# A streaming kernel whose engine programs are shortened: waits and counts folded into arithmetic instructions, PE's groups in a loop, masks moved to Pool

## The chip, the cores and the metric

The kernel runs on one core of a Trainium2 chip. The metric is the device time of one execution in microseconds (us). Every run quoted here is fast: it lies within 1.5% of the fastest run of the same kernel. The engines are called VectorE (DVE in the profiles), ScalarE (ACT), Pool, PE (the matrix engine) and SyncE (SP); they wait for each other by semaphores, which are counters. Data is moved by 16 DMA engines. Comparisons are between kernels run on the same chip, except where the text says so.

## The reference

```python
def reference(x, w):                                # x: 8 x 2048 x 4096, w: 4096 x 1, float32
    proj = (x @ w).squeeze(-1)                      # 8 x 2048
    cm = np.maximum.accumulate(proj, axis=1)
    is_record = (proj >= cm).astype(np.float32)
    return np.cumsum(is_record, axis=1).astype(np.float32)
```

x holds 268 MB and is read once. Everything else is small.

## The kernel before

The rows of x are worked on in four groups, of 4, 4, 4 and 3 rows per partition, and a tail of 128 rows per batch. A group has eight tiles, one per batch. A tile is 128 partitions by `r` rows of 4096 numbers: 8.4 MB for a group of four rows, 6.3 MB for three. SyncE issues all loads of x, in order. Of each row VectorE multiplies and sums 2816 columns (one "dot"), Pool multiplies the other 1280 in place, and ScalarE sums what Pool wrote. When a tile is done, both VectorE and ScalarE have incremented its semaphore `fr[t]`, and the buffer may be loaded again. At the end of a group PE transposes the sums into PSUM, and VectorE runs the scans (maximum, comparison, count).

`at` picks the buffer by the tile's number within its group, since the engines run the groups as a loop and the same instruction must address the same buffer each time:

```python
NS = 3                                   # buffers; B = 8 tiles in a group, NL = 3 groups of four rows
def at(g, t):
    return xbuf[(t if g < NL else t + NS - 1) % NS]

def user_before(g, t):                   # whose release the load of tile t of group g waits for
    if t >= NS:
        return t - NS, g + 1
    if g == NL:
        return B - NS + t, g
    return max(u for u in range(B) if u % NS == t), g
```

The VectorE side, where a tile's wait also tells Pool to go, and the Pool side:

```python
def group_dots(r, g=0):                                   # VectorE
    for t in range(B):
        b, xb = B - 1 - t, at(g, t)
        V.wait_ge(xs[t], 16).then_inc(go, 1)              # landed; Pool may go
        V.sem_inc(xs[t], -16)
        for j in range(r):
            i = dot(xb[:, j * D : j * D + VC], w_v[:, :VC], sum_v[...])
        i.then_inc(fr[t], 1)
...
with V.Fori(0, NL - 1):                                   # two turns of a loop,
    next_group()
    group_dots(R)
next_group()                                              # a third copy written out
group_dots(R)
...
def group_products(r, g=0):                               # Pool
    for t in range(B):
        for j in range(r):
            xl = at(g, t)[:, j * D + VC : (j + 1) * D]
            i = G.tensor_mul(out=xl, in0=xl, in1=w_sb).then_inc(pl, 1)
            if j == 0:
                i._wait_ge(go, 1)
        G.sem_inc(go, -1)
```

In the tail the pieces of the last 128 rows run through the same three engines. Each sum is spread over batches by a small mask instruction (on ScalarE, the last one on VectorE) and added up on PE. Before the very last dot VectorE waits until ScalarE has done its last sum.

Of the kernel before, what the change touches and what calls it, by code (L numbers as in the profile page):

```python
# [13 lines left out]
ALU = mybir.AluOpType  # L14
ACTF = mybir.ActivationFunctionType
NEG = -3.0e38
LOW = -3.2e38
# [3 lines left out]
def kernel(  # L21
# [16 lines left out]
    P = 128  # L38
    B, S, D = x.shape
# [18 lines left out]
    LAST = [  # L58
        (B - 2, 1696, D, (1696, VC), (VC, D)),
        (B - 2, 0, 1696, (0, 1696), None),  # L60
        (B - 1, 2592, D, (2592, 3552), (3552, D)),
        (B - 1, 1440, 2592, (1792, 2592), (1440, 1792)),
        (B - 1, 736, 1440, (736, 1184), (1184, 1440)),
        (B - 1, 352, 736, (352, 736), None),
        (B - 1, 0, 352, (0, 352), None),
    ]
# [3 lines left out]
    TILES = [(m, 0, D, (0, VC), (VC, D)) for m in range(B - 2)] + LAST  # L70
    NP = sum(q[0] == B - 1 for q in LAST)
    EARLY = 4
    W2, W2C = 1184, 608

    pool = ctx.enter_context(tc.tile_pool(name="sb", bufs=1))
    wpool = ctx.enter_context(
# [37 lines left out]
    def sem(name):  # L114
        return tc.alloc_semaphore(f"{name}_{next(ns)}")
# [1 line left out]
    xs = [sem("xs") for _ in range(B)]  # L117
    fr = [sem("fr") for _ in range(B)]
    xq = [sem("xq") for _ in TILES]
    ws, idn, bw, wc, cs, od, oe, psr, pd, pl, go, sd, pa, con, fo, ms = (  # L120
        sem(n) for n in "ws idn bw wc cs od oe psr pd pl go sd pa con fo ms".split()
    )

    V, A, G, T, SY = nc.vector, nc.scalar, nc.gpsimd, nc.tensor, nc.sync
# [31 lines left out]
    def user_before(g, t):  # L156
# [3 lines left out]
            return B - NS + t, g  # L160
        return max(u for u in range(B) if u % NS == t), g

    with tc.tile_critical(no_gpsimd_drain=True):  # L163

        for g in range(NG):
            r = RS[g]
            for t in range(B):
                i = SY.dma_start(
                    out=at(g, t)[:, : r * D],
                    in_=x[B - 1 - t, STARTS[g] : STARTS[g] + r * P, :].rearrange(  # L170
                        "(p r) d -> p (r d)", r=r
                    ),
                ).then_inc(xs[t], 16)
                u, n = user_before(g, t)
                if n:
                    i._wait_ge(fr[u], 2 * n)
                if g == t == 0:
                    A.dma_start(
                        out=w_row, in_=w.rearrange("(k c) one -> k (c one)", k=NW)
                    ).then_inc(ws, 16)  # L180
                if t == 4 and g:
                    SY.dma_start(
                        out=out[:, STARTS[g - 1] : STARTS[g]], in_=cnt
                    )._wait_ge(cs, g + 1).then_inc(od, 16)
# [9 lines left out]
        for i, (m, c0, c1, _, _) in enumerate(TILES):  # L194
            u, xb = slot(m)
            d = SY.dma_start(  # L196
                out=xb[:, c0:c1],
                in_=x[
                    rows_of(m)[0] : rows_of(m)[0] + H,
                    S0 + rows_of(m)[1] : S0 + rows_of(m)[1] + Q, c0:c1,  # L200
                ].rearrange("b i d -> i b d"),
            ).then_inc(xq[i], 16)
            if u not in freed:
                freed.add(u)
                d._wait_ge(fr[u], 2 * NG)
            if i == len(TILES) - 4:
                SY.dma_start(
                    out=out[:, STARTS[-1] : S0], in_=cnt[:, : S0 - STARTS[-1]]
                )._wait_ge(cs, NG + 1).then_inc(oe, 16)
# [12 lines left out]
        for n, k in enumerate(order):  # L222
            c = k * WC
            dst = w_v[:, c : c + WC] if c < CV else ps
            i = T.matmul(  # L225
                out=dst, lhsT=identity[:NW, k : k + 1].to_broadcast([NW, P]),
                rhs=w_row, start=True, stop=True,
            ).then_inc(bw, 1)
            if n == 0:
                i._wait_ge(ws, 16)  # L230
        A.copy(out=w_sb[:, CV - VC :], in_=ps)._wait_ge(bw, 1).then_inc(wc, 1)  # L231
        A.copy(out=w_sb[:, : CV - VC], in_=w_v[:, VC:CV])._wait_ge(bw, NW).then_inc(  # L232
            wc, 1
        )
        A.copy(out=w2, in_=w_v[:, W2 : W2 + W2C]).then_inc(wc, 1)  # L235
        A.sem_inc(od, 32)


        V.wait_ge(idn, 1)
        V.memset(by_b, 0.0).then_inc(fo, 1)  # L240
        V.wait_ge(fo, 1)
        V.tensor_reduce(
            out=by_b[:, B - H : B], in_=identity.rearrange("p (i b) -> p b i", b=H),
            op=ALU.add,
            axis=mybir.AxisListType.X,
        )
        V.tensor_reduce(
            out=by_i, in_=identity.rearrange("p (i b) -> p i b", b=H), op=ALU.add,
            axis=mybir.AxisListType.X,
        ).then_inc(fo, 1)  # L250
        V.wait_ge(fo, 2)
        V.memset(cm[:, N - 1 :], NEG)
        V.memset(cnt[:, N - 1 :], 0.0)
        V.wait_ge(con, 3)
        V.wait_ge(wc, 3)
        V.memset(ps[:B, :N], LOW).then_inc(psr, 1)  # L256

        def group_scans(r=R):
            V.wait_ge(od, 16)
            n = r * P  # L260
            scans(cm[:, :n], cnt[:, :n], ps[:B, :n], cm[:, N - 1 :], cnt[:, N - 1 :])

        def group_dots(r, g=0):
            for t in range(B):
                b, xb = B - 1 - t, at(g, t)
                V.wait_ge(xs[t], 16).then_inc(go, 1)
                V.sem_inc(xs[t], -16)  # L267
                for j in range(r):
                    i = dot(
                        xb[:, j * D : j * D + VC], w_v[:, :VC],  # L270
                        sum_v[:, j * B + b : j * B + b + 1],
                    )
                i.then_inc(fr[t], 1)

        def next_group():
            group_scans()
            V.sem_inc(psr, -3)
            V.sem_inc(od, -16)

        with V.Fori(0, NL - 1):  # L280
            next_group()
            group_dots(R)
        next_group()
        group_dots(R)
        next_group()
        group_dots(RS[-1], NL)

        def group_products(r, g=0):
# [13 lines left out]
        def group_sums(r, g=0):  # L302
            for t in range(B):
                b = B - 1 - t
                for j in range(r):
                    i = add_up(
                        at(g, t)[:, j * D + VC : (j + 1) * D],
                        sum_p[:, j * B + b : j * B + b + 1],
                    )._wait_ge(pl, j + 1)
                i.then_inc(fr[t], 1)  # L310
                A.sem_inc(pl, -r)
            A.wait_ge(pd, 1)
            A.sem_inc(pd, -1)

        with A.Fori(0, NL):
            group_sums(R)
        group_sums(RS[-1], NL)

        for g, r in enumerate(RS):
            for j in range(r):  # L320
                for k, l in enumerate((sum_p, sum_v)):
                    i = T.matmul(  # L322
                        out=ps[:B, j : r * P : r], lhsT=l[:, j * B : (j + 1) * B],
                        rhs=identity, start=k == 0, stop=k == 1,
                    )
                    if j == k == 0:
                        i._wait_ge(fr[B - 1], 2 * (g + 1))
                    if j == r - 1:
                        i.then_inc((pd, psr)[k], 1)


        nv = npool = na = nm = 0

        def sums(i, dst_v, dst_p):
            nonlocal nv, npool, na
            m, _, _, v, p = TILES[i]
            xb = slot(m)[1]
            dot(xb[:, v[0] : v[1]], w_v[:, v[0] : v[1]], dst_v)._wait_ge(
                xq[i], 16
            ).then_inc(sd, 1)  # L340
            nv += 1
            if p:
                xl = xb[:, p[0] : p[1]]
                G.tensor_mul(out=xl, in0=xl, in1=w_pool(*p))._wait_ge(  # L344
                    xq[i], 16
                ).then_inc(pl, 1)
                npool += 1
                add_up(xl, dst_p)._wait_ge(pl, npool).then_inc(pa, 1)
                na += 1

        def by_batch(m, acc, start, stop, *wait):
            nonlocal nm
            e = masked[:, nm * B : (nm + 1) * B]
            b, q = rows_of(m)
            on = by_b[:, B - H - b : 2 * B - H - b]
            if m < B - 1:
                A.activation(out=e, in_=on, func=ACTF.Copy, scale=acc)._wait_ge(  # L357
                    *wait
                ).then_inc(ms, 1)
            else:  # L360
                V.tensor_tensor(
                    out=e, in0=on, in1=acc.to_broadcast([P, B]), op=ALU.mult
                )._wait_ge(*wait).then_inc(ms, 1)
            nm += 1
            return T.matmul(  # L365
                out=ps[:B, q : q + Q], lhsT=e, rhs=by_i, start=start, stop=bool(stop),
            )._wait_ge(ms, nm)

        def tail_scans(m0, m1, cm0, cnt0, base):
            a, b = (m * H * Q // B for m in (m0, m1))  # L370
            scans(cm_l[:, a:b], cnt_l[:, a:b], ps[:B, a:b], cm0, cnt0, base)

        A.wait_ge(fo, 2)
        n = RS[-1] * P
        for i, (m, c0, _, _, p) in enumerate(TILES[: -NP]):
            dv = acc_v[:, i : i + 1]
# [11 lines left out]
                tail_scans(0, EARLY, cm[:, n - 1 : n], cnt[:, n - 1 : n], 4)  # L388
        for j in range(NP):
            i = len(TILES) - NP + j  # L390
            if j == NP - 1:
                V.wait_ge(pa, na)
            sums(i, accs[:, j : j + 1], accs[:, NP + j : NP + j + 1])
        V.tensor_reduce(
            out=fin, in_=accs, op=ALU.add, axis=mybir.AxisListType.X
        )._wait_ge(sd, nv).then_inc(sd, 1)
# [36 lines left out]
```

## Time and profile before

The kernel before takes 633.26 us (median of 4 runs, 633.20 to 633.31).

The next lines are from the page of the kernel before. In the rows of digits each digit is the busy share of one fortieth of the span, in tenths; then come the DMA queues with packets, MB and their share of sixteen engines' time.

```profile
span 631.6 us, 1212 instructions
...
DVE  0755676456785557755579655577557866655797
...
POOL 0554676456765557755567655577555866555865
...
DMA  9999999999999999999999999999999999999995
...
q1 hardware_dynamic: 6560, 268.50, 98.6%
q14 instruction: 4, 0.03, 0.0%
q8 instruction: 1, 0.02, 0.0%
```

The DMA row is full from start to end: the kernel is bound by the load of x. VectorE (64%) and Pool (58%) have time to spare. The instruction queues carry almost nothing, five packets.

The timeline of the kernel before around the end of the first group, near 140 us: start, duration, engine, line, operation, and in brackets how long the engine had been idle. SPq is the issue of a load by SyncE.

```profile
140.19 11.50 POOL L292 TENSOR_TENSOR xall<-xall,w_sb 128x1280 f32<-128x1280 f32 x4 [7.86 <-POOLq L295]
140.33 3.09 DVE L127 CUSTOM_DVE_ANT_0 xall<-xall,w_v 128x2816 f32<-128x2816 f32 x1 [7.23 <-DVEq L267]
...
151.72 1.27 ACT L133 ACTIVATE xall<-xall 128x1280 f32<-128x1280 f32 x1 [1.50 <-POOL xall L292]
...
153.11 0.33 SPq L168 DMA_DIRECT2D xall<-in_x_dram  x1
```

A tile has landed at 140.06; Pool and VectorE start at once, ScalarE's last sum ends near 153.1, and in that moment SyncE issues the next load into the same buffer. So a buffer is free 13 us after landing. A tile takes 19.35 us to load.

The end of the kernel before, by the timeline: the scans of the last group, the last dot, and the reduction that starts the final chain.

```profile
599.52 1.00 DVE L143 TENSOR_TENSOR_SCAN cm<-ps,cm,small 8x384 f32<-8x384 f32 x1 [0.58 <-PE ps L322]
...
626.60 0.52 DVE L127 CUSTOM_DVE_ANT_0 xall<-xall,w_v 128x352 f32<-128x352 f32 x1 [0.35 <-ACT xall L133]
...
627.16 0.17 DVE L394 TENSOR_REDUCE small<-small 128x1 f32<-128x10 f32 x1
```

The last piece of x landed at 626.02 (the trace's landing records), and the reduction follows 1.14 us later.

### The profile page before, as it was taken

Reading aid. Unit: us, or ns where it says so; the run is one execution under the profiler, and the core shown is the slowest. Engines: PE = TensorE matmul, PEld = TensorE weight load, DVE = VectorE, ACT = ScalarE, POOL = GpSimd, SP = SyncE. Lnnn points to the kernel's source line nnn. Section 1 sums busy time; section 2 is a strip of 40 time slices with the busy share of each in tenths; the row PEclk is TensorE's granted clock in tenths of the full one; section 3 lists DMA queues with packets and bytes.
Section 4 is the critical chain, followed back from the end, with each engine's and each line's share of the span. In section 5 each row is a group of like instructions: output and inputs, shape, how many; then the busy total and the mean of one; then the engine's idle time right before and its main releaser. Section 6 shows DMA issues by size and latency. Waiting matters only on the chain.

```text
span 631.6 us, 1212 instructions
## 1 busy us (share of the span) xinstructions
PE 32.3 (5%) x108; PEld 14.4 (2%) x108; DVE 407.0 (64%) x295; ACT 182.0 (29%) x279; POOL 369.1 (58%) x138
## 2 busy tenths in 40 slices
PE   8000000000010000000020000000002000000111
PEld 3000000000000000000010000000001000000000
DVE  0755676456785557755579655577557866655797
ACT  1222332123322233222233222332222332322353
POOL 0554676456765557755567655577555866555865
PEclk9999999999999999999996555555556555555555
DMA  9999999999999999999999999999999999999995
GB/s 400 403 461 398 465 398 461 403 465 398 465 432 432 448 415 452 412 457 407 457 407 457 407 457 407 462 403 461 403 459 420 431 442 439 415 442 418 428 423 204
DMA packets 6581, 268.57 MB, mean 425 GB/s; under 512 B 768, under 2 KB 1040, under 8 KB 1584
## 3 DMA queue, kind: packets, MB, share of 16 engines
q1 hardware_dynamic: 6560, 268.50, 98.6%
q14 instruction: 4, 0.03, 0.0%
q8 instruction: 1, 0.02, 0.0%
q10 hardware_dynamic: 16, 0.02, 0.0%
HBM read 268.45 MB, written 0.07 MB: 425 GB/s over the span
## 4 chain that ended last, share of the span: by engine, by line
POOL 52%; issue 37%; DMA 7%; PE 2%; SPq 0%; DVE 0%; ACT 0%; POOLq 0%; ACTq 0%; DVEq 0%
POOL xall L292 52%; DMA xall<-in_x_dram 6%; PE w_v L225 2%; PE ps L225 0%; SPq L196 0%; DMA w<-in_w_dram 0%; POOL xall L344 0%; POOLq L295 0%; ACT xall L133 0%; ACT w L235 0%; DVE xall L127 0%; PE ps L365 0%; DVE cm_l L143 0%; DVE cnt_l L149 0%; DVE ps L146 0%
## 5 line engine op out<-in xcount | busy, mean ns | idle before, releaser
L127 DVE CUSTOM_DVE_ANT_0 xall<-xall,w_v 128x2816 f32<-128x2816 f32 (+3 forms) x133 | 388.4, 2973 | 190.1 <-DVEq L267 187.9
L292 POOL TENSOR_TENSOR xall<-xall,w_sb 128x1280 f32<-128x1280 f32 x120 | 344.8, 2903 | 248.5 <-POOLq L295 248.5
L133 ACT ACTIVATE xall<-xall 128x1280 f32<-128x1280 f32 (+1 forms) x130 | 162.9, 1253 | 425.5 <-POOL xall L292 415.1
L322 PE MATMUL ps<-identity,small 128*8 128x128 f32 x60 | 13.1, 409 | 569.7 <-ACT xall L133 569.7
L344 POOL TENSOR_TENSOR xall<-xall,w_sb 128x1280 f32<-128x1280 f32 (+1 forms) x8 | 21.6, 2709 | 7.3 <-DMA xall<-in_x_dram 7.3
L133 ACT ACTIVATION_READ_ACCUMULATOR xall<-xall 128x1 f32 x130 | 24.2, 186 | 0.0
L322 PEld LDWEIGHTS ps<-identity,small 128*8 128x8 f32 x60 | 7.4, 129 | 576.5 <-ACT xall L133 572.5
L143 DVE TENSOR_TENSOR_SCAN cm<-ps,cm,small 8x512 f32<-8x512 f32 (+1 forms) x5 | 6.1, 1218 | 13.2 <-PE ps L322 13.2
L225 PE MATMUL w_v<-w,identity 8*128 8x512 f32 x14 | 12.2, 1056 | 0.0
L256 DVE MEMSET ps<- 8x512 f32 x1 | 0.5, 485 | 16.0 <-ACT w L235 16.0
L127 DVE DVE_READ_ACCUMULATOR2_ANT small<- 128x1 f32 x133 | 10.8, 81 | 0.0
L365 PE MATMUL ps<-fold,masked 128*8 128x64 f32 x32 | 5.2, 299 | 23.3 <-ACT masked L357 17.3
L149 DVE TENSOR_TENSOR_SCAN cnt<-ps,cnt,small 8x512 f32<-8x512 f32 (+1 forms) x5 | 6.1, 1217 | 0.2
L357 ACT ACTIVATE masked<-fold,small 128x8 f32<-128x8 f32 x15 | 4.0, 296 | 4.1 <-DVE small L127 3.9
L225 PEld LDWEIGHTS w_v<-w,identity 8*128 8x128 f32 x14 | 4.6, 332 | 7.3 <-issue 7.3
L232 ACT COPY w_sb<-w_v 128x768 f32<-128x768 f32 x1 | 0.8, 798 | 11.4 <-PE w_v L225 11.4
L146 DVE TENSOR_TENSOR ps<-ps,cm 8x512 f32<-8x512 f32 (+1 forms) x5 | 3.3, 660 | 0.2
L365 PEld LDWEIGHTS ps<-fold,masked 128*8 128x8 f32 x32 | 1.9, 97 | 26.8 <-ACT masked L357 19.8
L225 PE MATMUL ps<-w,identity 8*128 8x512 f32 x2 | 2.1, 1136 | 2.6 <-DMA w<-in_w_dram 2.6
L231 ACT ACT_TABLE_LOAD x1 | 1.3, 1283 | 1.6 <-SPq L163 1.6
L344 POOL TENSOR_TENSOR xall<-xall,w 128x352 f32<-128x352 f32 (+1 forms) x2 | 1.6, 841 | 0.1
L231 ACT COPY w_sb<-ps 128x512 f32<-128x512 f32 x1 | 0.6, 585 | 1.9 <-PE ps L225 1.9
(22 smaller groups left out, 5.4 us busy)
## 6 DMA issues: line engine op xcount, KB each, us to landing
xall<-in_x_dram SPq DMA_DIRECT2D x8, 6144.0 KB, 33.5
xall<-in_x_dram SPq DMA_DIRECT2D x6, 2048.0 KB, 42.5
xall<-in_x_dram SPq DMA_DIRECT2D x1, 1200.0 KB, 36.7
xall<-in_x_dram SPq DMA_DIRECT2D x1, 848.0 KB, 38.1
xall<-in_x_dram SPq DMA_DIRECT2D x1, 752.0 KB, 39.3
xall<-in_x_dram SPq DMA_DIRECT2D x1, 576.0 KB, 40.1
xall<-in_x_dram SPq DMA_DIRECT2D x24, 45.1
xall<-in_x_dram SPq DMA_DIRECT2D x1, 352.0 KB, 22.5
```

The costliest lines, as they stand in the source:

```text
L127: return V.tensor_tensor_reduce(out=xsl, in0=xsl, in1=wsl, scale=1.0, scalar=0.0, op0=ALU.mult, op1=ALU.add, accum_out=dst,)
L133: return A.activation(out=xsl, in_=xsl, func=ACTF.Copy, accum_out=dst)
L143: V.tensor_tensor_scan(out=cm_, data0=src, data1=low, initial=cm0, op0=ALU.max, op1=ALU.max,)._wait_ge(psr, base).then_inc(psr, 1)
L146: V.tensor_tensor(out=src, in0=src, in1=cm_, op=ALU.is_ge)._wait_ge(psr, base + 1).then_inc(psr, 1)
L149: V.tensor_tensor_scan(out=cnt_, data0=src, data1=low, initial=cnt0, op0=ALU.add, op1=ALU.max,)._wait_ge(psr, base + 2).then_inc(cs, 1)
L225: i = T.matmul(out=dst, lhsT=identity[:NW, k : k + 1].to_broadcast([NW, P]), rhs=w_row, start=True, stop=True,).then_inc(bw, 1)
L231: A.copy(out=w_sb[:, CV - VC :], in_=ps)._wait_ge(bw, 1).then_inc(wc, 1)
L292: i = G.tensor_mul(out=xl, in0=xl, in1=w_sb).then_inc(pl, 1)
L322: i = T.matmul(out=ps[:B, j : r * P : r], lhsT=l[:, j * B : (j + 1) * B], rhs=identity, start=k == 0, stop=k == 1,)
L344: G.tensor_mul(out=xl, in0=xl, in1=w_pool(*p))._wait_ge(xq[i], 16).then_inc(pl, 1)
L357: A.activation(out=e, in_=on, func=ACTF.Copy, scale=acc)._wait_ge(*wait).then_inc(ms, 1)
L365: return T.matmul(out=ps[:B, q : q + Q], lhsT=e, rhs=by_i, start=start, stop=bool(stop),)._wait_ge(ms, nm)
```

## The change

Its intent is shorter engine programs. VectorE's separate wait and count instructions go into the arithmetic instructions beside them, and one such pair of ScalarE's becomes one instruction; VectorE runs the full groups as three turns of a loop instead of two and a copy; PE runs its groups in a loop, and the buffer of a group's last tile is given back through PE (semaphore `p7`), which also takes over VectorE's wait for the output of the counts (`od`); Pool makes six of the early masks of the tail; the wait for ScalarE moves from before the last dot to after it; and the split of two tail pieces shifts, by 32 and by 64 columns. The core of the diff:

```diff
-                V.wait_ge(xs[t], 16).then_inc(go, 1)
-                V.sem_inc(xs[t], -16)
                 for j in range(r):
                     i = dot(...)
+                    if j == 0:
+                        i._wait_ge(xs[t], 16).then_inc(go, 1)
+                    elif j == 1:
+                        i.then_inc(xs[t], -16)
                 i.then_inc(fr[t], 1)
...
-        with V.Fori(0, NL - 1):
-            next_group()
-            group_dots(R)
-        next_group()
-        group_dots(R)
-        next_group()
+        with V.Fori(0, NL):
+            group_scans()
+            V.sem_inc(psr, -3)
+            group_dots(R)
...
-        for g, r in enumerate(RS):
+        def group_rows(r):
+            T.wait_ge(fr[B - 1], 2).then_inc(p7, 1)
+            T.sem_inc(fr[B - 1], -2)
+            T.wait_ge(od, 16).then_inc(od, -16)
             ... (the matmuls of a group)
+        with T.Fori(0, NL):
+            group_rows(R)
+        group_rows(RS[-1])
...
+            pool = m < B - 2 and wait[0] is sd
+            if pool:
+                G.tensor_tensor(
+                    out=e, in0=on, in1=acc.to_broadcast([P, B]), op=ALU.mult
+                )._wait_ge(*wait).then_inc(mg, 1)
...
-            if j == NP - 1:
-                V.wait_ge(pa, na)
             sums(i, accs[:, j : j + 1], accs[:, NP + j : NP + j + 1])
+        V.wait_ge(pa, na)
```

More of the change, by code (lines that the diff above doesn't have):

```diff
@@ L60 @@
         (B - 2, 0, 1696, (0, 1696), None),
-        (B - 1, 2592, D, (2592, 3552), (3552, D)),
+        (B - 1, 2592, D, (2592, CV), (CV, D)),
         (B - 1, 1440, 2592, (1792, 2592), (1440, 1792)),
-        (B - 1, 736, 1440, (736, 1184), (1184, 1440)),
+        (B - 1, 736, 1440, (736, 1248), (1248, 1440)),
         (B - 1, 352, 736, (352, 736), None),
@@ L72 @@
     EARLY = 4
-    W2, W2C = 1184, 608
+    W2, W2C = 1248, 544
     pool = ctx.enter_context(tc.tile_pool(name="sb", bufs=1))
@@ L119 @@
     xq = [sem("xq") for _ in TILES]
-    ws, idn, bw, wc, cs, od, oe, psr, pd, pl, go, sd, pa, con, fo, ms = (
-        sem(n) for n in "ws idn bw wc cs od oe psr pd pl go sd pa con fo ms".split()
+    ws, idn, bw, wc, cs, od, oe, psr, pd, pl, go, sd, pa, con, fo, ms, p7, mg = (
+        sem(n) for n in "ws idn bw wc cs od oe psr pd pl go sd pa con fo ms p7 mg".split()
     )
@@ L161, in user_before, with free @@
         return max(u for u in range(B) if u % NS == t), g
+    def free(u, n):
+        return (p7, n) if u == B - 1 else (fr[u], 2 * n)
     with tc.tile_critical(no_gpsimd_drain=True):
@@ L175 @@
                 if n:
-                    i._wait_ge(fr[u], 2 * n)
+                    i._wait_ge(*(free(u, n)))
                 if g == t == 0:
@@ L204 @@
                 freed.add(u)
-                d._wait_ge(fr[u], 2 * NG)
+                d._wait_ge(*free(u, NG))
             if i == len(TILES) - 4:
@@ L230 @@
                 i._wait_ge(ws, 16)
+        A.wait_ge(fo, 2).then_inc(od, 16)
         A.copy(out=w_sb[:, CV - VC :], in_=ps)._wait_ge(bw, 1).then_inc(wc, 1)
@@ L235 @@
         A.copy(out=w2, in_=w_v[:, W2 : W2 + W2C]).then_inc(wc, 1)
-        A.sem_inc(od, 32)
-        V.wait_ge(idn, 1)
-        V.memset(by_b, 0.0).then_inc(fo, 1)
-        V.wait_ge(fo, 1)
+        V.memset(by_b, 0.0)._wait_ge(idn, 1).then_inc(fo, 1)
         V.tensor_reduce(
             out=by_b[:, B - H : B], in_=identity.rearrange("p (i b) -> p b i", b=H),
-            op=ALU.add,
-            axis=mybir.AxisListType.X,
-        )
+            op=ALU.add, axis=mybir.AxisListType.X,
+        )._wait_ge(fo, 1)
         V.tensor_reduce(
@@ L250 @@
         ).then_inc(fo, 1)
-        V.wait_ge(fo, 2)
-        V.memset(cm[:, N - 1 :], NEG)
-        V.memset(cnt[:, N - 1 :], 0.0)
-        V.wait_ge(con, 3)
-        V.wait_ge(wc, 3)
-        V.memset(ps[:B, :N], LOW).then_inc(psr, 1)
+        V.memset(cm[:, N - 1 :], NEG)._wait_ge(fo, 2)
+        V.memset(cnt[:, N - 1 :], 0.0)._wait_ge(con, 3)
+        V.memset(ps[:B, :N], LOW)._wait_ge(wc, 3).then_inc(psr, 1)
         def group_scans(r=R):
-            V.wait_ge(od, 16)
             n = r * P
@@ L272, in group_dots @@
                     )
+                    if j == 0:
+                        i._wait_ge(xs[t], 16).then_inc(go, 1)
+                    elif j == 1:
+                        i.then_inc(xs[t], -16)
                 i.then_inc(fr[t], 1)
-        def next_group():
+        with V.Fori(0, NL):
             group_scans()
             V.sem_inc(psr, -3)
-            V.sem_inc(od, -16)
-        with V.Fori(0, NL - 1):
-            next_group()
             group_dots(R)
-        next_group()
-        group_dots(R)
-        next_group()
+        group_scans()
+        V.sem_inc(psr, -3)
         group_dots(RS[-1], NL)
@@ L311, in group_sums @@
                 A.sem_inc(pl, -r)
-            A.wait_ge(pd, 1)
-            A.sem_inc(pd, -1)
+            A.wait_ge(pd, 1).then_inc(pd, -1)
         with A.Fori(0, NL):
@@ L325 @@
                     )
-                    if j == k == 0:
-                        i._wait_ge(fr[B - 1], 2 * (g + 1))
                     if j == r - 1:
                         i.then_inc((pd, psr)[k], 1)
-        nv = npool = na = nm = 0
+        with T.Fori(0, NL):
+            group_rows(R)
+        group_rows(RS[-1])
+        nv = npool = na = nm = on_a = on_g = 0
         def sums(i, dst_v, dst_p):
@@ L351, in by_batch @@
         def by_batch(m, acc, start, stop, *wait):
-            nonlocal nm
+            nonlocal nm, on_a, on_g
             e = masked[:, nm * B : (nm + 1) * B]
@@ L355, in by_batch @@
             on = by_b[:, B - H - b : 2 * B - H - b]
-            if m < B - 1:
+            pool = m < B - 2 and wait[0] is sd
[3 more added lines that the diff above has]
+                )._wait_ge(*wait).then_inc(mg, 1)
+            elif m < B - 1:
                 A.activation(out=e, in_=on, func=ACTF.Copy, scale=acc)._wait_ge(
@@ L364, in by_batch @@
             nm += 1
+            if pool:
+                on_g += 1
+            else:
+                on_a += 1
             return T.matmul(
                 out=ps[:B, q : q + Q], lhsT=e, rhs=by_i, start=start, stop=bool(stop),
-            )._wait_ge(ms, nm)
+            )._wait_ge(*((mg, on_g) if pool else (ms, on_a)))
         def tail_scans(m0, m1, cm0, cnt0, base):
@@ L371, in tail_scans @@
             scans(cm_l[:, a:b], cnt_l[:, a:b], ps[:B, a:b], cm0, cnt0, base)
-        A.wait_ge(fo, 2)
         n = RS[-1] * P
```

## The prediction

> **What bounds the kernel now.** The load of x. In the page's slices the DMA row reads 9 from first to last; q1 moves 268.5 MB at a mean of 425 GB/s, 98.6% of sixteen engines' span. The Trainium skill, "DMA: Bandwidth & Descriptors", section "Where 436 GB/s comes from", puts the port ceiling at 435 GB/s; the trace agrees (425). VectorE is busy 64%, Pool 58%, ScalarE 29%. By the timeline a steady tile of 4 rows lands every 19.4 us, and its buffer is free about 13 us after landing (four dots 12.1 us; four Pool products 11.5 us plus one ScalarE sum 1.5 us). Three buffers rotate, so a whole tile is always queued behind the one in flight. Only start and tail can therefore move the time: the last x lands near 626.0 us (estimate: 737 KB at 425 GB/s after 624.2), and the final chain follows.
>
> **What the change does.** Mid-stream it removes sequencer instructions, which sit in waits (VectorE sits idle 188 us before dots). It saves no stream time. The groups on PE as a loop move nothing. DVE's program shrinks from 235 to 168 rows in the instruction order.
>
> The important move is hidden: `go`, which releases Pool, was incremented by VectorE's wait as soon as the tile landed (Pool starts 0.14 us before the dot). Now it hangs on the first dot, and that inc sits on its accumulator read, 3.1 us later (dot 3.02 us start to start, read 0.08). Pool and ScalarE thus run 3.1 us later on every tile (more after a group's scans). Buffers come free about 16 us after landing instead of 13; within 19.4, and 13.2 within 14.5 for three-row tiles. The stream shouldn't notice.
>
> **The tail should.** Last group's last tile: the first dot starts at 586.8, so Pool starts at 589.95 instead of 586.67 and ends at 598.6; ScalarE ends at 599.8 (596.5 before); the twelve row matmuls take 2.75 us; the scans start at 602.95 instead of 599.52, with VectorE idle meanwhile. VectorE then has 22.7 us of back-to-back work; its old waits (0.9 + 0.63 + 0.31 us) absorb part, and taking the wait for ScalarE off the last dot gives back about 0.35. Last dot done at about 628.2 instead of 627.1.
>
> Pool's masks now wait for the dots: the mask of the sixth batch pair waits until about 621.6, so the next product runs 621.85 to 624.75 (before about 618.9 to 621.8). ScalarE's sum, three masks and three last sums follow in order: 626.15, 626.85, 627.6, 628.2, 628.65. VectorE's final wait clears at about 628.75; the final reduce, at 627.16 before, starts at about 628.8. Mask, matmul, scans and output are unchanged. Sum: +1.65 us, all on the final chain; the smaller last pieces (256 to 192 columns) are in that sum.
>
> **Prediction: 634.9 us, range 634.0 to 635.6.** Chance of faster by over 2%: 0.5%; within 2%: 99%; slower by over 2%: 0.5%.
>
> **What the profile would show.** DMA row unchanged, about 425 GB/s, last x piece landing at the same time. Pool's first product about 3.1 us after VectorE's first dot of each tile. VectorE idle some 4 us before the last group's scans, starting near 603. No DMA waits of VectorE from batch pair 5 on. The final reduce near 628.8, with ScalarE's last sum just ahead of it.
>
> **What would make it wrong.** If `go` rises at the first dot's start, the tail is about 0.3 us shorter than before: 633.0. If the later freeing of buffers makes a gap in the stream, it costs microseconds more. If Pool's small masks take over half a microsecond, or ScalarE's queue is slower than I added up, the tail grows further. Another chip's DMA rate could move both kernels.

## The result

The changed kernel takes 637.06 us (median of 4 runs, 636.89 to 637.42) against 633.26 of the kernel before: 3.8 us slower. The ratio is 1.0061, 95% interval 1.0043 to 1.0078. (A ratio here is the mean time of one kernel's fast runs over the mean of the other's in the same rounds, so not quite the ratio of the medians.) That is above the range of the prediction, 634.0 to 635.6, though well within 2%.

The page of the changed kernel, the same lines:

```profile
span 635.6 us, 1158 instructions
...
DVE  0855677455776557755568655676555986555787
...
POOL 0355775457736577555574655765457586665776
...
DMA  9999999999999999999999999999999999999994
...
q1 hardware_dynamic: 6560, 268.50, 98.2%
...
q14 instruction: 3, 0.02, 0.0%
```

The same bytes took a longer span, and two instruction packets are gone. The row of digits still looks full; a loss of 4 us in 635 can't be seen in it. The landing times of the tiles show it. This table is worked out from the trace's landing records; a tile has landed when its sixteenth increment is there.

```
                                         before     changed
last tile of group 1 landed at           159.42      158.90
first tile of group 2 after it           +19.34      +21.35
last tile of group 2 landed at           314.32      315.87
first tile of group 3 after it           +19.35      +21.54
last tile of group 3 landed at           469.22      473.16
first, second tile of group 4      +14.53, +15.50    +14.51, +14.54
last tile of group 4 landed at           586.54      589.43
last piece of x landed at                626.02      628.85
final reduction starts                   627.16      631.18
```

So the stream lost 2 us where group 2 begins and 2 us where group 3 begins, and won 1 us early in group 4; in group 1 the two traces differ by half a microsecond the other way. The tail after the last landing grew from 1.14 to 2.33 us. These sum up to 3.9 of the 4.0 us between the two spans.

The timeline of the changed kernel at the end of the first group:

```profile
139.58 3.09 DVE L127 CUSTOM_DVE_ANT_0 xall<-xall,w_v 128x2816 f32<-128x2816 f32 x1 [7.24 <-DMA xall<-in_x_dram]
142.75 11.48 POOL L285 TENSOR_TENSOR xall<-xall,w_sb 128x1280 f32<-128x1280 f32 x4 [7.88 <-POOLq L288]
...
154.26 1.27 ACT L133 ACTIVATE xall<-xall 128x1280 f32<-128x1280 f32 x1 [1.48 <-POOL xall L285]
...
155.65 0.33 SPq L171 DMA_DIRECT2D xall<-in_x_dram  x1
```

Pool starts 3.17 us after VectorE's first dot, where before it started 0.14 us ahead of it, and the next load is issued 16.1 us after the tile landed (139.56), not 13. The rate of the stream in the two stretches that hold the borders, first of the kernel before and then of the changed one: start and end, duration, busy us (and number of instructions) of PE, PE's weight loads, VectorE, ScalarE and Pool, and at the end the granted clock, the DMA share and GB/s. A packet's bytes count in the stretch in which it starts, so single stretches can exceed what the engines can move; the comparison is between the kernels.

```profile
155.00:185.00 30.00, 3.58 (x16) 1.97 (x16) 20.95 (x14) 7.14 (x11) 17.60 (x7) 1.00 1.04 450
...
305.00:345.00 40.00, 3.58 (x16) 2.04 (x16) 28.38 (x20) 11.00 (x18) 24.25 (x9) 0.87 1.02 442
```

```profile
155.00:185.00 30.00, 3.57 (x16) 1.98 (x16) 18.00 (x12) 6.08 (x10) 11.47 (x4) 1.00 1.00 419
...
305.00:345.00 40.00, 3.57 (x16) 2.05 (x16) 24.72 (x18) 9.54 (x14) 20.33 (x8) 1.00 1.00 419
```

At both borders between groups the rate falls. The packet records of the trace show why. How many of the 16 DMA engines had a packet in work, worked out from the starts and durations of the packets (mean of the quarter of a microsecond that begins there):

```
us               157.25  157.75  158.25  158.75  159.25
before             16.0    16.1    16.0    16.0    16.0
changed            16.0    12.0    11.0    14.6    16.0
```

In the changed kernel the first engines finish their part of the last tile of group 1 at 157.35. The next load was issued at 155.65, 1.7 us earlier, and its packets are not there for all of them: five engines stand still, the longest until 159.26. The first packets that they then move are slow: 2.5 to 3.6 us for 64 KB instead of 2.42. At the border to group 3 (312.9 to 314.0 us) it is worse, with as few as 6 of 16 at work.

The standing still is the smaller part of the loss. Near 160 us all 16 engines are at work again, and most packets still take 2.7 to 2.8 us. Added up over the engines (156 to 185 and 311 to 341 us), 17 us of engine time went in standing still and 33 us in packets that took longer than the usual 2.42 (64 KB) or 1.82 us (48 KB); in the kernel before both sums are nil, within 0.5 us. So here an issue that came too late cost more than the gap that it left.

The end of the changed kernel:

```profile
605.87 1.00 DVE L143 TENSOR_TENSOR_SCAN cm<-ps,cm,small 8x384 f32<-8x384 f32 x1 [4.30 <-PE ps L317]
...
630.50 0.50 DVE L127 CUSTOM_DVE_ANT_0 xall<-xall,w_v 128x352 f32<-128x352 f32 x1
...
630.63 0.35 ACT L133 ACTIVATE xall<-xall 128x192 f32<-128x192 f32 x1
...
631.18 0.16 DVE L398 TENSOR_REDUCE small<-small 128x1 f32<-128x10 f32 x1 [0.17 <-ACT xall L133]
```

VectorE waits 4.30 us for the last group's sums, which come late because Pool started late, and then works without a pause to the end of its last dot. ScalarE's last sum and VectorE's last dot end within 0.2 us of each other.

### The profile page after: what moved, and what is told of

Its sections match the earlier page's. It is cut to its first block, busy times and chain, and to the rows that moved or that the text cites. A ratio compares the mean times of both kernels' runs of the same rounds, so it can differ in the third digit from the quotient of the medians.

```text
span 635.6 us, 1158 instructions
## 1 busy us (share of the span) xinstructions
PE 32.2 (5%) x108; PEld 15.0 (2%) x108; DVE 406.6 (64%) x295; ACT 180.1 (28%) x273; POOL 369.2 (58%) x144
## 3 DMA queue, kind: packets, MB, share of 16 engines
HBM read 268.45 MB, written 0.07 MB: 422 GB/s over the span
## 5 line engine op out<-in xcount | busy, mean ns | idle before, releaser
L371 PEld LDWEIGHTS ps<-fold,masked 128*8 128x8 f32 x32 | 2.4, 110 | 24.0 <-ACT masked L359 16.1
L359 ACT ACTIVATE masked<-fold,small 128x8 f32<-128x8 f32 x9 | 2.5, 297 | 0.2
```

Source lines behind the costliest of these rows:

```text
L359: A.activation(out=e, in_=on, func=ACTF.Copy, scale=acc)._wait_ge(*wait).then_inc(ms, 1)
L371: return T.matmul(out=ps[:B, q : q + Q], lhsT=e, rhs=by_i, start=start, stop=bool(stop),)._wait_ge(*((mg, on_g) if pool else (ms, on_a)))
```

## The experiments

The theory: `go` now hangs on the completion of the first dot, so Pool, ScalarE and the release of every buffer are 3.1 us late. Within a group this costs nothing, since three tiles lie between two uses of a buffer and a whole tile is queued. But 8 is not a multiple of 3: tiles 7 and 8 of a group use the buffers that tiles 1 and 2 of the next group need, so at the border only two tiles lie between two uses, and there the release comes just before the DMA engines run out. The rivals: the hop of the last buffer's release over PE (`p7`), the loop on PE, and the masks on Pool. Names that begin with "a" are the changed kernel with an edit, those with "b" the kernel before with an edit. All results were correct.

### a1: go at the wait again

```diff
+                V.wait_ge(xs[t], 16).then_inc(go, 1)
                 for j in range(r):
                     i = dot(...)
-                    if j == 0:
-                        i._wait_ge(xs[t], 16).then_inc(go, 1)
-                    elif j == 1:
+                    if j == 1:
                         i.then_inc(xs[t], -16)
```

> The changed kernel with one thing undone: go is raised by VectorE's wait again, as soon as the tile landed; everything else of the change stays. Theory (buffers freed 3 us later starve the DMA queue where groups meet, about 2 us at each of the first two group borders, and the late Pool delays the tail): the border tiles land 19.4 us after the tile in front of them again, not 21.4 and 21.5, and the time falls from 637.1 to about 632.0 (631.4 to 632.6), below the kernel before, since one pair of instruction fetches less is in the stream. Rival (the extra hop over PE before the second buffer is given back, the PE loop, or Pool's masks): stays above 636.

Measured: 631.81 us (631.56 to 632.13), before 633.29, ratio 0.9975 (0.9959 to 0.9992). The first tiles of groups 2 and 3 land 19.34 and 19.35 us after the tile in front of them. One instruction per tile given back removes the whole loss, at the borders and in the tail, and the rest of the change is then worth 1.5 us in the other direction.

### b1: only the late go, in the kernel before

```diff
-                V.wait_ge(xs[t], 16).then_inc(go, 1)
-                V.sem_inc(xs[t], -16)
                 for j in range(r):
                     i = dot(...)
+                    if j == 0:
+                        i._wait_ge(xs[t], 16).then_inc(go, 1)
+                    elif j == 1:
+                        i.then_inc(xs[t], -16)
```

> The kernel before with only this part of the change: the wait moves into the first dot, go hangs on the first dot, the reset on the second. Theory (late go is the cause): both borders lose about 2 us of stream, the time is 637 to 638.5. Rival (PE hop, PE loop, masks): stays at 633.3.

Measured: 636.39 us (634.54 to 636.87), ratio 1.0042 (1.0023 to 1.0061). The borders lose 1.5 and 1.7 us in its trace. The late go alone makes the kernel before slow, though the loss is smaller than I expected: 3.1 us by the medians, not 4 to 5. Its trace says why in part: the second tile of each next group loses another 0.4 and 0.0 us and the tail 0.5 (1.66 us after the last landing), but 1.0 us comes back in group 4, whose second tile takes 14.54 us here and not 15.50.

### a2 and a3: masks back on ScalarE; PE written out, no hop

```diff
# a2
-            pool = m < B - 2 and wait[0] is sd
+            pool = False
# a3
-        return (p7, n) if u == B - 1 else (fr[u], 2 * n)
+        return (fr[u], 2 * n)
-            T.wait_ge(fr[B - 1], 2).then_inc(p7, 1)
-            T.sem_inc(fr[B - 1], -2)
+            T.wait_ge(fr[B - 1], 2 * (g + 1))
-        with T.Fori(0, NL):
-            group_rows(R)
-        group_rows(RS[-1])
+        for g, r in enumerate(RS):
+            group_rows(g, r)
```

> The changed kernel with the early masks back on ScalarE. Theory: the stream doesn't know of them, and in the tail VectorE's dots and ScalarE's sums end within 0.1 us of each other, so at most 0.3 us is gained: 636.8 to 637.2. Rival (Pool, waiting for dots, holds the tail): under 636.2.

> The changed kernel with PE's groups written out again, and the loads waiting on the sum semaphore itself and not on PE's hop. Theory (late go): 636.7 to 637.3, borders still lose about 2 us each. Rival (the hop over PE gives the buffer back late): about 633 to 635.

Measured: a2 636.25 us (633.78 to 637.15), a3 635.96 us (634.92 to 637.00). Both medians miss the expected ranges, and both kernels scatter widely, over 3.4 and 2.1 us; the kernels that lose nothing at the borders stay within 1.0 us. In the trace of a2 the first tiles after the borders are still 1.2 and 1.6 us late, in that of a3 1.1 and 0.5 (and the second tiles another 0.2 and 0.45), and the final reduction follows the last landing by 2.13 us in a2 against 2.33 in the changed kernel. So neither part is the cause. The times can't tell from the scatter whether the hop over PE makes the border a little worse, but the traces can. The load that comes late at a border, that of tile 1, waits for tile 7's own semaphore and not for `p7` (see `user_before`): it is issued 16.1 us after tile 7 landed with the hop (changed) and without it (a3, b1). Only the load of tile 2 waits for `p7`: it is issued 16.18 and 16.19 us after tile 8 landed, against 16.10 in a3. The hop costs 0.1 us, and not where the loss begins.

### a4: the late go stays, the buffers rotate across the borders

```diff
-        return xbuf[(t if g < NL else t + NS - 1) % NS]
+        return xbuf[(g * B + t) % NS]
-        if g == NL:
-            return B - NS + t, g
-        return max(u for u in range(B) if u % NS == t), g
+        return B - NS + t, g
-        with V.Fori(0, NL):                       # and the same for ScalarE and Pool
+        for g in range(NL):
```

> The changed kernel, go still late, but the three buffers rotate on across the group borders (VectorE's, ScalarE's and Pool's loops are written out for it), so that three tiles lie between two uses of a buffer at the border too, instead of two. Theory (short reuse distance at the border times late freeing): the border tiles land 19.4 us after the tile in front of them; about 4 us come back, up to 1.5 us go to more instruction fetches, the tail keeps its 1.2 us: 633.5 to 635. Rival (late go slows every tile, or costs in another way): stays at 637.

Measured: 634.44 us (634.28 to 634.85), before 633.47, ratio 1.0019 (1.0002 to 1.0035). The first tiles of groups 2 and 3 land 19.34 and 19.35 us after the tile in front of them. Pool is as late as in the changed kernel; what changed is the distance between two uses of a buffer, and the length of three programs whose loops are written out, which brings more instruction fetches (seven on queue 14 instead of three). What is left of the loss against the kernel before is no more than the longer tail (2.26 us after the last landing against 1.14). This is the cleanest evidence for the border. The stretch from 155 to 185 us, as above:

```profile
155.00:185.00 30.00, 3.57 (x16) 1.97 (x16) 18.01 (x12) 6.07 (x10) 11.49 (x4) 1.00 1.04 452
```

### a5: the late go stays, Pool has less to do

```diff
-    VC = 2816
+    VC = 3136
```

> The changed kernel, go still late, with 3136 columns for VectorE and 960 for Pool instead of 2816 and 1280, so that buffers come free near 13.5 us after landing in spite of the late go (estimate: four dots of 3.35 us; Pool 3.4 us late, then 8.7 us of products and 1.2 us of sum). Theory: no loss at the borders. VectorE has 11% more to do in the tail, which costs there 1 to 2 us, so the landing times tell and not the time: about 634 to 636. Rival (the go itself, whatever the freeing): borders still lose 2 us each, time 638 or more.

Measured: 632.98 us (632.89 to 633.27), ratio 0.9994 (0.9978 to 1.0011), 1.0 us below the expected range: the longer tail that I had expected didn't come, the reduction follows the last landing by 2.14 us against 2.33 in the changed kernel. SyncE issues the load at the first border at 153.21 us, and both borders land at 19.35. Go is even later than in the changed kernel (Pool starts 3.5 us after the first dot, not 3.17), but the buffer is free early, and nothing is lost. It is the release that counts.

### b2a, b2b and b2c: early go, a late release of chosen buffers

```diff
                     )._wait_ge(pl, j + 1)
+                late = g < NL and t >= B - 2      # b2b: t < B - 2; b2c: one repeat, not two
+                for k in range(2 * late):         # ScalarE repeats the tile's last sum
+                    i.then_inc(dl, 1)
+                    i = add_up(...)._wait_ge(dl, k + 1)
+                if late:
+                    A.sem_inc(dl, -2)
                 i.then_inc(fr[t], 1)
```

> The kernel before, go early, but in the three full groups ScalarE repeats the last sum twice for the tiles 7 and 8 of a group, so that only these two buffers, the ones used again two tiles later, come free 2.9 us later. The last group and the tail are as before. Theory: each of the first two borders loses about 2 us of stream: 636.5 to 638. Rival (late go matters otherwise than by freeing buffers): 633.3.

> The kernel before, go early, with the same delay of 2.9 us for the other six tiles of a full group, whose buffers are used again three or more tiles later. Theory: a whole tile is queued there, nothing is lost: 633.0 to 633.6. Rival (any late freeing costs stream time): over 635.

> As b2a, with one repeated sum instead of two: the two buffers come free about 1.45 us later than in the kernel before, a load is issued some 2.8 us before the first DMA engine runs out of work, between 4.2 (no loss) and 1.9 (loss). Theory: a loss between none and that of b2a: 633.2 to 634.3; it tells where the lead becomes too short.

Measured: b2a, two tiles of eight late, 634.71 us (634.14 to 635.45), ratio 1.0025 (1.0008 to 1.0041); b2b, the other six late, 633.01 us (632.85 to 633.63), ratio 0.9997 (0.9981 to 1.0014); b2c, half the delay, 632.91 us (632.81 to 633.42), ratio 0.9993 (0.9977 to 1.0008). The direction is as expected for b2a and b2b, and only the reuse at the border is sensitive. The size of b2a is smaller than I expected (1.2 us instead of 3 or more): its first border lost 1.7 us, its second 0.8 over two tiles, and 1.0 us came back in group 4 as in b1. b2c lost nothing where I had expected a little. The three delays can be read as a lead, that is the time from the issue of the first load of group 2 to the moment at which the first DMA engine runs out of the old tile (both from the traces):

```
kernel                  issue    first engine done   lead   first tile of group 2 late by
before                 153.11         157.91          4.8         0.0
b2c (half delay)       154.15         157.36          3.2         0.0
b2a (full delay)       155.43         157.40          2.0         1.7
b1  (late go)          155.78         157.53          1.7         1.5
changed                155.65         157.35          1.7         2.0
```

A lead of 3.2 us is enough here and one of 2.0 us is not. The kernel before had a reserve of less than 2.8 us, and the change spent 3.1. (The lateness is against the 19.35 us of a steady tile.) Below that the lead doesn't give the size of the loss: at the second border of the kernels that starve it is 0.3 to 0.9 us, and the first tile is 2.2 us late in the changed kernel (lead 0.3), 1.7 in b1 (0.3) and only 0.2 in b2a (0.6).

### a6 and a1 again: are the masks on Pool worth anything, and does a1 beat the kernel before?

> a1 (go at the wait) with the early masks on ScalarE again as well. Theory: with go early neither engine holds the end, VectorE's last dot does; within 0.2 us of a1, 631.6 to 632.0. Rival (the masks on Pool help, as the change meant them to): over 632.2.

> a1 once more, on the same chip as b3 and a6, with more rounds, to see whether it beats the kernel before beyond doubt: 631.5 to 632.1, before 633.0 to 633.6.

a6 is a1 with the edit of a2. Measured with 5 rounds on one chip: a1 631.84 us (631.73 to 632.27), a6 631.85 us (631.73 to 632.22), before 633.53; both ratios 0.9975 (0.9961 to 0.9988). The masks on Pool gain nothing. a1 is faster than both kernels: 1.7 us less than the kernel before by the medians, 0.25% by the ratio. Its end, by the timeline:

```profile
624.97 0.52 DVE L127 CUSTOM_DVE_ANT_0 xall<-xall,w_v 128x352 f32<-128x352 f32 x1
...
625.53 0.16 DVE L397 TENSOR_REDUCE small<-small 128x1 f32<-128x10 f32 x1
```

The last piece landed at 624.78, so the reduction follows 0.75 us later instead of 1.14: the 0.35 us that the last dot waited for ScalarE are gone (this part of the change wasn't tried alone). The other 1.2 us are in the stream: 1.0 in group 4, where the prediction had said that a shorter program saves nothing, and 0.3 in group 1, where the kernels differ by up to 0.7 us in no clear order.

### b3, b4, a7 and a8: what the length of a program costs

The landing table shows a tile of the kernel before that took 15.50 us instead of 14.53, the second of group 4. The packet records (start, end, duration in us; bytes; queue; other engines' packets left out) show two fetches of instructions in that time. The records don't name the DMA engine; by their times the first joins these data packets, and only these:

```
490.539 492.357 took 1.818 size 49152 q1
492.353 492.686 took 0.333 size 8192 q14
492.674 495.153 took 2.479 size 49152 q1
```

The fetch takes 0.33 us and the data packet behind it 0.66 longer than the usual 1.82, so this engine is 1.0 us later from then on. The delay is not made up: from the first to the last of a tile's sixteen increments it is 1.17 us at the first tile of group 4, 2.13 us at the second, and still 2.24 us at the end of the stream. These four kernels vary the programs alone:

```diff
# b3 (kernel before): VectorE's third copy goes into the loop
-        with V.Fori(0, NL - 1):
+        with V.Fori(0, NL):
             next_group()
             group_dots(R)
-        next_group()
-        group_dots(R)
# b4: b3, and the reset of the landing semaphore goes onto the second dot
-                V.sem_inc(xs[t], -16)
+                    if j == 1:
+                        i.then_inc(xs[t], -16)
# a7: a1, with waits that are already satisfied, at the start, where VectorE is idle
+        V.wait_ge(idn, 1)
+        for _ in range(64):
+            V.wait_ge(idn, 1)
# a8: a1 with PE's groups written out, the edit of a3
```

> The kernel before with one change: VectorE's loop runs the full groups three times, instead of twice with a third copy written out, so VectorE's program falls from 236 to about 169 rows of the instruction order. Theory (the two instruction fetches at 492 and 493 us, which stop a DMA engine for a good 0.7 us each, are this longer program's): the pair is gone, the second tile of the last group lands 14.5 us after the first and not 15.5, and the time is 632.2 to 632.6. Rival (the 1.5 us by which the changed kernel with early go beats the kernel before come from the tail or from chance): 633.1 to 633.5.

> b3 and the reset of the landing semaphore folded into the second dot, go still raised by the wait: VectorE's program is 202 instructions, b3 218, a1 196. Theory: the fetch that b3 had at 604 us moves behind the end of the stream, the stream ends about 1 us earlier than in b3, at 625.0, and since the last dot still waits for ScalarE the time is 632.2 to 632.7. Rival: 633.2 to 633.6 like b3.

> a1 (go at the wait) with waits that are already satisfied in front of VectorE's first memset, where VectorE has 16 us to spare, so that its program is as long again as that of b3 (229 instructions, b3 218, a1 196) with no more work. Theory (program length costs stream time by instruction fetches that stop one DMA engine): one more fetch before the stream ends, near 600, and 631.8 to 633.0, +1 us if it hits the engine that lands last. Rival (length of VectorE's program is worth nothing): as a1, 631.6 to 632.0, with the same fetches.

> a1 with PE's groups written out again. In all kernels with these groups written out the traces have a fetch of 16 KB near 619 us that takes 1.07 us on one DMA engine, in those with the loop none. Theory: the fetch is back; the time is a1's if it hits an engine that is ahead (631.6 to 632.0), up to 1 us more if it hits the last one.

Measured: b3 633.43 us (before 633.53, ratio 0.9999, 0.9986 to 1.0013); b4 632.76 us (before 633.31, ratio 0.9990, 0.9976 to 1.0003); a7 632.51 us (ratio 0.9988, 0.9974 to 1.0002); a8 632.50 us (ratio 0.9986, 0.9973 to 1.0000). b3 and the second a1 ran on one chip, the other three and the first a1 on another; between these the kernel before moved by 0.2 us. Against the kernel before none of these four ratios is clear of 1; what follows rests on the landings in the traces, and on runs that don't overlap (a1 at most 632.27 us, a7 at least 632.48, a8 at least 632.42; b4 at most 633.06, b3 at least 633.27).

The expectation for b3 fell, and its trace says how: of the pair at 492 and 493 us one fetch is gone and the tile takes 14.54 us, but a fetch appears at 604 us, so b3's stream ends at 626.09, as late as that of the kernel before. Sixteen instructions less (b4) move that fetch to 627 us, behind the end of the stream, which then ends at 625.38, and 0.4 to 0.7 us are won (0.45 by the medians against the kernel before of the same call, 0.6 by the ratios, 0.7 by the medians as they are). Padding a1 with idle waits (a7) brings one in at 590 us, and 0.7 us are lost (against the first a1, on the same chip). Writing out PE's groups (a8) brings back one of 16 KB that takes 1.09 us at 617 us, and again 0.7 us are lost. The count of instruction packets on the page, first of a1 (its second run), then of a8:

```profile
q14 instruction: 3, 0.02, 0.0%
```

```profile
q8 instruction: 1, 0.02, 0.0%
q14 instruction: 3, 0.02, 0.0%
```

All nine kernels with PE's groups written out (before, a3, a8 and the six of b) have the packet on queue 8 in their traces, and none of the seven with the loop has. So the intent of the change was right: each of the two shorter programs can be worth 0.4 to 0.7 us. It isn't additive, and a fetch in the stream doesn't always cost: b3 saved instructions and nothing else; in b2a a pair of fetches at 496.69 and 498.06 us delayed no tile of group 4 (14.53 and 14.54 us each); and in the kernel before the fetch on queue 8 at 618.88 left the time from the last tile of group 4 to the last piece at 39.48 us, as in a1 (39.49), where there is none. That it depends on whether the fetch hits the DMA engine that is last anyway is a guess, since the records don't name the engine.

## Why the prediction was wrong

- **"The load of x bounds the kernel"**: right. The trace shows 433 to 434 GB/s while all 16 engines are at work, close to the 435 GB/s that the Trainium skill names in "DMA: Bandwidth & Descriptors", section "Where 436 GB/s comes from". The same passage says that for transfers between HBM and SBUF the HBM side binds, at about 358 GB/s; this load from HBM (the page of the profile counts 268.45 MB read there) ran at a mean of 425, so here the measurement decides.
- **"Go hangs on the first dot, Pool runs 3.1 us later"**: right, 3.17 us in the trace. The Trainium skill, "Perfetto Trace Analysis", section "The 4-stage abstract model", puts the semaphore update after the execution, and the trace agrees. Folding a signal that follows a wait into an instruction that does work delays it by that work.
- **"Buffers come free about 16 us after landing"**: right, 16.1 us at 155.65.
- **"Three buffers rotate, so a whole tile is always queued behind the one in flight. Only start and tail can therefore move the time"**: this is the step that failed, and with it "the stream shouldn't notice". It holds within a group. At the first two borders the buffers of tiles 7 and 8 are used again two tiles later. There I should have compared 16 us not with "within 19.4", but with 19.4 less the 1.5 us by which the first DMA engine is done before a tile has landed, and less the lead that a load needs. The reserve of the kernel before was under 2.8 us, the change took 3.1, and each border lost about 2 us. The source told it, in `user_before`; and the third border, where `at` shifts the rotation, lost nothing. The prediction had this case among its risks ("a gap in the stream"), but left it out of its range.
- **"It saves no stream time; the groups on PE as a loop move nothing"**: wrong, in the other direction. The shorter programs can take instruction fetches out of the stream, 0.4 to 0.7 us each for VectorE's (b3 to b4, a1 to a7) and PE's (a1 to a8). In the changed kernel the second tile of group 4 took 14.54 us and not 15.50. Whether its time would have been longer without the shorter programs isn't shown: a3, which takes PE's loop back, wasn't slower within its scatter.
- **The tail, +1.65 us**: the mechanism was right and the size a bit high; it measured 1.19 us (2.33 less 1.14). The early part came out as added up: the scans started 16.44 us after the last group's last landing, predicted 16.41, with VectorE idle for 4.30 us. Over half of the difference lies in ScalarE's last three sums, which took 1.5 us and not 1.8.
- **The views named in advance**: Pool's late start, VectorE's idle time before the scans and the missing waits in the tail came as said. The mean rate fell from 425 to 423 GB/s, and the last piece of x landed 2.8 us later; these two said where the miss was.

What stays open: why the packets after a gap are slow, which is two thirds of the engine time lost at the borders, why the loss doesn't follow the lead, and why most kernels that starve scatter by 1 to 3 us (the changed kernel itself only by 0.5).

## What to carry to other kernels

When a stream bounds the kernel, find the shortest distance between two uses of a buffer, above all at loop borders where the tile count is not a multiple of the buffer count, and hold the release time against that one, with the lead that a load needs (here between 2.0 and 3.2 us). A signal that was given at a wait should not move to the end of an instruction that works for 3 us just to save one instruction; keep the signal on a wait and fold the resets, which nobody waits for, as a1 does. Shorter programs can pay in a kernel bound by DMA, since instruction fetches stood in the way of its data packets here, but look up in the trace where the fetches fall before expecting anything.

## What the Trainium skill lacked or had wrong

- "Runtime: NRT & Kernel Launch", section "Instruction fetch mechanics", says that crossing a block of instructions costs one bump of a DMA queue's tail, mostly hidden. VectorE doesn't notice it here (its dots run without a pause around the fetches at 492 and 493 us), but the stream can: in the kernel before a fetch of 8 KB took 0.3 to 0.4 us, and the data packet behind it 0.25 to 0.7 us longer (2.95 and 2.67 instead of 2.42 us, 2.48 and 2.15 instead of 1.82). One fetch more in the stream cost 0.7 us of the kernel's time in a7 and in a8; the pair in b2a delayed no tile.
- "DMA: Bandwidth & Descriptors", section "Queues, rings and completion order", puts the refill of instructions on row 14. Here 8 KB packets of kind "instruction" ran on queue 14, and one of 16 KB, of 1.07 to 1.09 us, on queue 8 in every kernel with PE's groups written out.
- "DMA: Bandwidth & Descriptors", section "Anatomy of one DMA", gives about 2.0 us of fixed cost, on the path that Pool issues, and puts most of it after the last byte. No page that I read says how early SyncE must issue a load, behind one that is still running, so that the engines don't run dry, or that packets slow down after they did: a lead of 3.2 us lost nothing, one of 2.0 us lost 1.7 us on an 8.4 MB tile. With 1.7 us of lead the last engine got its first packet 3.6 us after the issue, and the first packets after the gap took up to 3.6 us instead of 2.42.
